# The first two gate/up tiles of each feed-forward layer by the plain product, and the operands of the seven-product form made on VectorE in overlapped chains

## The chip, the cores and the metric

The kernel runs on one core of one Trainium2 chip, as one program. The metric is the device time of one execution in microseconds (us); the median of 3 runs of the kernel before is 3172.42 us (3166.53 to 3172.50).

The engines are named as in the profile: PE is the matrix engine (TensorE), PEld its loading of the fixed operand, DVE the vector engine, ACT the scalar engine with the activation functions, POOL the GpSimd engine, SP the engine whose queue issues most DMA transfers. Each takes its instructions in the order of its own list, and a wait holds up all that stands behind it on that engine. Matrix products are written to PSUM banks, everything else lies in SBUF.

## The reference

One step of a two-layer network over 1024 latent tokens and 128 context tokens, 1152 in all, with 1024 features. Layer 0 mixes tokens by differential attention, layer 1 by a long convolution, and each is followed by the same feed-forward part, which is all that this change touches:

```python
def swiglu(h, w_gu, w_down):
    g, u = jnp.split(h @ w_gu, 2, axis=-1)
    return (jax.nn.silu(g) * u) @ w_down

h = modulate(rmsnorm(xs, norm2_g[i]), sh2, sc2)      # normalised, scaled and shifted by features
xs = xs + g2 * swiglu(h, ffn_w_gu[i], ffn_w_down[i])
```

`w_gu` is 1024 x 5632: 2816 gate columns and 2816 up columns. All is in float32.

## The kernel before, in words

**Precision.** PE multiplies a 32-bit format with a shorter mantissa, so every operand is kept as two parts: `hi`, a copy rounded by ACT, and `lo`, the rest, by a subtraction (`part`, lines 1635 to 1637). A product is three matrix products, hi*hi, lo*hi and hi*lo (`three`, lines 304 to 307).

**The stage.** `gate_up` (line 969) makes silu(gate)*up for 22 tiles of 128 gate columns with their 128 up columns, for each of the two layers, and stores them to DRAM (`d_a`). The 1152 tokens are two halves of 576 and the 1024 features two halves of 512, so that a pair of tiles is a 2x2 block of weights (gate and up by feature halves) times a 2x2 block of activations (feature halves by token halves). From tile 2 on (the loop in line 1141) that block product takes seven products of a 512x128 weight with a 512x576 activation in place of eight, in a Strassen-Winograd form. Line 1002 lists them: the numbers 1 to 7 are the products (`p1` to `p7`), the letters `a`, `b`, `c` the PSUM banks in which they add up. One product is 24 matrix products of 288 columns (4 feature tiles, 2 column halves, 3 parts; `times`, line 962). The loop body is p1, p6, p2, p7, p5, p4, p3.

**Operands.** The seven products need sums of weight blocks (`side_sums`, on POOL) and of activation blocks. `aa` and `bb` are the lower feature half for the first and second token half, `dd` and `ee` the upper one. Needed are, each as hi and lo, all 4x128 features by 576 tokens: `low` (b0, b1: aa and dd, first token half), `right` (t4: bb, second token half, lower features), `ops[3]` (b2: ee, second token half, upper features), and the combinations t2 = ee - (bb - aa), t3 = t2's sum minus aa, t1 = bb - aa, and a second t4 = dd - t2's sum. The combinations overwrite aa, bb, dd and ee in place, so their order matters.

**The opening of the stage** is where the order is written out by hand, and the call of `pin` in line 1193 keeps the order of the code on PE, DVE, ACT and POOL. The activations of the last third of tokens (256 latents and 128 context tokens, chunk c = 2, all in the second token half) still wait for the norm (`rstd_parts`) and for `apply` (line 891: a DVE product with the norm, then scale and shift on ACT, and on POOL for the context columns). Until they are there only the first token half can be multiplied. Therefore tile 0 is done plainly: `gate` and `up` with the first token half, 4 products of 24, then with the second, 4 more. Tile 1 is done by the seven products: its p1 runs beside tile 0's first pass, then the others follow as t2, t3, t1 and t4 come.

**Shared places.** Three PSUM banks of name `pr` go round (`bank`, line 995): the fourth product group waits until the first bank has been read out, by ACT (copy or silu) or by DVE. Weight parts `wh` and `wl` have three buffers each, raw weights two (`side_two`, `side_load`). `kept` (line 1077) holds tile 0's results and has the buffer name t1l, which the lo part of t1 takes later; `early`, of name t1h, holds tile 1's weight sums.

## Time and profile before

| | |
|---|---|
| median of 3 runs | 3172.42 us (3166.53 to 3172.50) |
| the profiled execution | 3174.84 us |
| its span | 3172.9 us |
| PE busy | 3054.7 us, 96% of the span |
| DVE busy | 1914.8 us, 60% |
| ACT busy | 1175.3 us, 37% |
| POOL busy | 1017.6 us, 32% |
| mean granted clock of PE | 0.985 |
| opening of layer 0's gate/up stage (first product of tile 0 to first of tile 2) | 982.18 to 1058.62 us |
| the same in layer 1 | 2355.70 to 2433.40 us |

All times within the program are counted from the start of the span. A row of a timeline gives start, duration, engine, line, operation, output<-inputs by the program's names without buffer numbers, and in brackets the idle time of the engine ahead of it and who ended it. L1636 and L1637 are the ACT and the DVE half of `part`, L1251 is any addition, subtraction or product by `tt`, L893 and L900 are `apply`, L1096 is a silu in `close`, L305 to L307 are the three products. A table by stretches gives, per engine, busy microseconds and in parentheses the number of instructions, then the clock that PE was granted as a share of full speed.

### The profile page before, as it was taken

Reading aid. Unit: us, or ns where it says so; the run is one execution under the profiler, and the core shown is the slowest. Engines: PE = TensorE matmul, PEld = TensorE weight load, DVE = VectorE, ACT = ScalarE, POOL = GpSimd, SP = SyncE. Lnnn points to the kernel's source line nnn. Section 1 sums busy time; section 2 is a strip of 40 time slices with the busy share of each in tenths; the row PEclk is TensorE's granted clock in tenths of the full one; section 3 lists DMA queues with packets and bytes.
Section 4 is the critical chain, followed back from the end, with each engine's and each line's share of the span. In section 5 each row is a group of like instructions: output and inputs, shape, how many; then the busy total and the mean of one; then the engine's idle time right before and its main releaser. Section 6 shows DMA issues by size and latency. Waiting matters only on the chain.

```text
span 3172.9 us, 53324 instructions
## 1 busy us (share of the span) xinstructions
PE 3054.7 (96%) x21370; PEld 2977.7 (94%) x21370; DVE 1914.8 (60%) x3103; ACT 1175.3 (37%) x2264; POOL 1017.6 (32%) x886
## 2 busy tenths in 40 slices
PE   6899999999998899999999999999998999999998
PEld 5679989999998899999999999999998999999998
DVE  7866523888926645445544678876456454545555
ACT  3631123888825322223211443335644222222214
POOL 5744310444424434342000323131244443430003
PEclk9999999999999999999999999999999999999999
DMA  6665352444141222224555223345621222125311
GB/s 247 212 203 189 130 161 85 99 90 90 48 155 42 73 76 71 76 77 137 192 213 192 100 98 119 136 153 187 202 69 52 73 77 76 71 76 185 119 63 67
DMA packets 164495, 379.14 MB, mean 119 GB/s; under 512 B 17391, under 2 KB 80247, under 8 KB 161560
## 3 DMA queue, kind: packets, MB, share of 16 engines
q1 hardware_dynamic: 148872, 353.37, 33.9%
q10 hardware_dynamic: 13968, 17.65, 1.5%
q0 software_dynamic: 1408, 4.72, 0.4%
q8 instruction: 168, 2.75, 0.4%
q14 instruction: 79, 0.65, 0.1%
HBM read 278.94 MB, written 96.73 MB: 118 GB/s over the span
## 4 chain that ended last, share of the span: by engine, by line
PE 81%; DVE 6%; DMA 3%; ACT 2%; issue 2%; POOL 1%; SPq 0%; POOLq 0%; ACTq 0%; DVEq 0%
PE mm L305 13%; PE mm L306 13%; PE mm L307 13%; PE pr L305 10%; PE pr L307 10%; PE pr L306 10%; PE tr L791 4%; PE sc L765 2%; PE sc L766 2%; PE tr L782 2%; PE tr L368 1%; DMA zt<-d_z 1%; ACT xk L900 1%; PE tr L307 1%; PE tr L305 1%
## 5 line engine op out<-in xcount | busy, mean ns | idle before, releaser
L306 PE MATMUL mm<-hs,wh 128*128 128x384 f32 x1632 | 548.3, 336 | 0.4 <-POOL hs L469 0.3
L307 PE MATMUL mm<-hs,wl 128*128 128x384 f32 x1632 | 546.6, 335 | 0.0
L305 PE MATMUL mm<-hs,wh 128*128 128x384 f32 x1632 | 545.9, 336 | 0.0
L863 DVE SCALAR_TENSOR_TENSOR xk<-mm,ada,xk 128x192 f32<-128x192 f32 (+3 forms) x560 | 233.6, 453 | 337.4 <-PE mm L307 331.7
L1251 DVE TENSOR_TENSOR xk<-pr,xk 128x576 f32<-128x576 f32 x204 | 154.0, 755 | 392.7 <-PE pr L307 206.4
L420 POOL TENSOR_TENSOR nacc<-nacc,nsq 128x384 f32<-128x384 f32 x104 | 117.2, 1127 | 665.1 <-ACT nsq L416 663.3
L1251 POOL TENSOR_TENSOR xk<-xk,xk 128x576 f32<-128x576 f32 x96 | 139.1, 1449 | 558.7 <-DVE xk L1251 454.1
L306 PEld LDWEIGHTS mm<-hs,wh 128*128 128x128 f32 x1632 | 306.4, 188 | 4.7 <-issue 2.2
L305 PEld LDWEIGHTS mm<-hs,wh 128*128 128x128 f32 x1632 | 306.1, 188 | 3.4 <-DVE xk L863 1.8
L307 PEld LDWEIGHTS mm<-hs,wl 128*128 128x128 f32 x1632 | 306.5, 188 | 2.1 <-issue 0.6
L1636 ACT ACTIVATE wh<-raw 128x1024 fp32r<-128x1024 f32 x154 | 162.5, 1056 | 369.1 <-PE mm L306 322.7
L1637 DVE TENSOR_TENSOR wl<-raw,wh 128x1024 fp32r<-128x1024 f32 x148 | 186.7, 1262 | 54.6 <-ACT wh L1636 54.3
L1637 DVE TENSOR_TENSOR wl<-xk,wh 128x512 fp32r<-128x512 f32 x160 | 180.0, 1165 | 50.4 <-ACT wh L1636 50.4
L305 PE MATMUL mm<-hh,wh 128*128 128x384 f32 x576 | 193.7, 339 | 2.8 <-ACT hh L527 2.3
L306 PE MATMUL mm<-hl,wh 128*128 128x384 f32 x576 | 194.8, 338 | 0.7 <-DVE hl L528 0.7
L307 PE MATMUL mm<-hh,wl 128*128 128x384 f32 x576 | 195.0, 339 | 0.0
L772 DVE TENSOR_REDUCE nm<-sc 128x1 f32<-128x1152 f32 x128 | 173.6, 1357 | 33.5 <-PE sc L766 33.4
L774 ACT ACTIVATE pr<-sc,nm 128x1152 f32<-128x1152 f32 x128 | 156.6, 1223 | 14.3 <-DVE nm L772 7.6
L1061 ACT ACTIVATE xk<-xk 128x576 f32<-128x576 f32 x40 | 27.4, 686 | 352.2 <-DVE xk L1251 352.2
L765 PE MATMUL sc<-kk,qs 128*128 128x384 f32 x384 | 140.1, 365 | 3.3 <-ACT pr L774 3.3
L791 PE MATMUL tr<-v,at 128*128 128x128 f32 x1152 | 139.4, 275 | 0.5 <-ACT at L786 0.5
L647 POOL TENSOR_TENSOR pr<-pr,al 128x384 f32<-128x384 f32 x64 | 53.6, 837 | 260.1 <-DVE al L643 256.7
(398 smaller groups left out, 8900.2 us busy)
## 6 DMA issues: line engine op xcount, KB each, us to landing
raw<-w_gu SPq DMA_DIRECT2D x88, 512.0 KB, 3.5
araw<-ada_w SPq DMA_DIRECT2D x64, 512.0 KB, 4.0
d_a<-xk SPq DMA_DIRECT2D x84, 288.0 KB, 2.1
raw<-w_down SPq DMA_DIRECT2D x44, 512.0 KB, 3.5
araw<-d_a SPq DMA_DIRECT2D x36, 576.0 KB, 7.5
kk<-d_k SPq DMA_DIRECT2D x16, 1152.0 KB, 8.6
raw<-w_in SPq DMA_DIRECT2D x24, 512.0 KB, 3.4
hl<-ada_w SPq DMA_DIRECT2D x23, 512.0 KB, 6.8
```

The lines of the kernel that those rows point to most:

```text
L305: self.nc.tensor.matmul(out, ah, bh, start=first, stop=False, **kw)
L306: self.nc.tensor.matmul(out, ah, bl, start=False, stop=False, **kw)
L307: self.nc.tensor.matmul(out, al, bh, start=False, stop=last, **kw)
L420: nc.gpsimd.tensor_tensor(out=self.acc[c], in0=self.acc[c], in1=sq, op=ALU.add)
L765: nc.tensor.matmul(sc[:, c, :CH], lhs, kk[:, 0, p, ks], start=True, stop=False)
L772: nc.vector.tensor_reduce(out=nm, in_=sv, axis=AX.XY, op=ALU.max, negate=True)
L774: nc.scalar.activation(e.rearrange("p (a b) -> p a b", a=3), sv, AF.Exp, bias=nm, accum_out=st[hd][3][:, p, qt : qt + 1])
L791: self.nc.tensor.matmul(po[:, :P], at[:, b], v[:, b], start=b == 0, stop=b == 8)
L863: self.nc.vector.scalar_tensor_tensor(out=x, in0=ps[:, s:e], scalar=gate[:, d, g : g + 1], in1=x, op0=ALU.mult, op1=ALU.add)
L1251: (eng or self.nc.vector).tensor_tensor(out=o, in0=a, in1=b, op=op)
L1636: self.nc.scalar.activation(hi, x, AF.Copy)
L1637: (eng or self.nc.vector).tensor_tensor(out=lo, in0=x, in1=hi.bitcast(F32), op=ALU.subtract)
```

## The change

In `gate_up`, for both layers:

- Tile 1 is multiplied plainly too: eight products in place of seven, spread over the two token halves. The first pass over the first token half holds gate and up of tile 0 and gate of tile 1; the second pass holds gate and up of tile 0 on the second half; then come up of tile 1 on the first half, gate of tile 1 on the second, up of tile 1 on the second.
- Tile 1's weight sums (`sums(1)`, four POOL instructions) and their four splits go away, with the buffer `early`; its up weights are split as they are, 128x1024.
- The splits of the weights of tiles 0 and 1 take their lo part on DVE where they had it on POOL. The subtractions bb - aa and dd - ee are on DVE too, and were on POOL.
- The operands are formed by a helper `chain`, which places `apply` of piece j, the ACT copy of piece j-1 and the DVE subtraction of piece j-2 in one round. Silu and product of the finished tiles stand inside these chains at a given round.
- Tile 1's closing work (additions in p6, p7, p5, p4, p3 and the products on POOL) becomes two silus on ACT and two products on DVE; `copies` goes, since only its plain case is left.
- t1 and the second t4 are formed in chains after tile 1's last product. Nothing is changed from `pair(t, 3)` of tile 2 on.

```diff
         raws(0)
-        g11, g12 = self.side_two(st[0]["raw"][0], eng=pool)
-        u21, u22 = self.side_two(st[0]["raw"][1], eng=pool)
+        g = self.side_two(st[0]["raw"][0])
+        u = self.side_two(st[0]["raw"][1])
         raws(1)
-        pair(1, 1, pool)
+        g1 = self.side_two(st[1]["raw"][0])
         norm = self.rstd_parts(NCH - 1)
-        gate, up, one = bank(), bank(), st[1]
-        one["a"] = bank()
-        kept, early = (self.tl(tp, [P, 4, HALF], tag=n) for n in ("t1l", "t1h"))
-        sums(1, [early[:, j, 0:512] for j in range(4)])
+        gate, up, gate1 = bank(), bank(), bank()
+        kept = self.tl(tp, [P, 4, HALF], tag="t1l")
+        low = [ops[1], ops[2]]
+
+        def plain(out, w, b, *halves):
+            for n in range(2):
+                self.times(out, w[n], b[n], n == 0, halves or (0, 1))
+
         for h in range(2):
-            self.times(gate, g11, ops[1], True, [h])
-            self.times(gate, g12, ops[2], False, [h])
+            plain(gate, g, low, h)
             if h == 0:
                 next(norm)
-            self.times(up, u21, ops[1], True, [h])
-            self.times(up, u22, ops[2], False, [h])
+            plain(up, u, low, h)
             if h == 0:
                 rs = next(norm)
-            self.times(one["a"], one["w"][1], ops[1], True, [h])
+            plain(gate1, g1, low, h)
...
-        for k in range(4):
-            apply(NCH - 1, k, rs)
-        for k in range(4):
-            self.part(*act(right, k), bb[k])
-            tt(bb[k], bb[k], aa[k], LESS, pool)
-            apply(NCH - 1, k + 4, rs)
-        close(0, gate, up)
-        copies(one, "s1", AF.Copy, "nacc", 3)
-        for k in range(4):
-            self.part(*act(ops[3], k), ee[k])
-        gate, up = bank(), bank()
-        self.times(gate, g11, right, True)
-        self.times(up, u21, right, True)
-        self.times(gate, g12, ops[3], False)
-        self.times(up, u22, ops[3], False)
-        for k in range(4):
-            tt(ee[k], ee[k], bb[k], LESS)
-            self.part(*act(t2, k), ee[k])
-        pair(1, 2)
-        for k in range(4):
-            tt(aa[k], ee[k], aa[k], LESS)
-            self.part(*act(t3, k), aa[k])
-        for k in range(4):
-            tt(dd[k], dd[k], ee[k], LESS, pool)
-        close(1, gate, up)
-        pair(1, 3, pool)
+        def silu(n, ps):
+            nc.scalar.activation(flat(kept, n), ps, AF.Silu)
+
+        def close(t, n, ps):
+            tt(flat(kept, n), ps, flat(kept, n), MUL)
+            store(t, n % 2, flat(kept, n))
+
+        def chain(dst, src, pre=None, lag=1, at={}):
+            n = len(src)
+            for j in range(n + 2 * lag):
+                if j < n and pre:
+                    pre(j)
+                k = j - lag
+                if 0 <= k < n:
+                    nc.scalar.activation(dst[k][0], src[k], AF.Copy)
+                k -= lag
+                if 0 <= k < n:
+                    tt(dst[k][1], src[k], dst[k][0].bitcast(F32), LESS)
+                if j in at:
+                    at[j]()
+
+        def rows(*ops):
+            return [(t[0][:, k], t[1][:, k]) for t in ops for k in range(4)]
+
+        chain(rows(*high), bb + ee, lambda k: apply(NCH - 1, k, rs), 1, {5: lambda: silu(0, gate), 8: lambda: close(0, 0, up)})
+        silu(2, gate1)
+        gate, up = bank(), bank()
+        plain(gate, g, high)
+        plain(up, u, high)
+        u1 = self.side_two(st[1]["raw"][1])
+        raws(2)
+        for k in range(4):
+            tt(bb[k], bb[k], aa[k], LESS)
+        chain(rows(t2), ee, lambda k: tt(ee[k], ee[k], bb[k], LESS), 1, {2: lambda: silu(1, gate), 4: lambda: close(0, 1, up)})
+        ups = bank()
+        plain(ups, u1, low)
+        gate1 = bank()
+        plain(gate1, g1, high)
+        pair(2, 1)
+        chain(rows(t3), aa, lambda k: tt(aa[k], ee[k], aa[k], LESS), 1, {4: lambda: close(1, 2, ups)})
+        sums(2)
+        silu(3, gate1)
+        ups = bank()
+        plain(ups, u1, high)
+        pair(2, 2)
+        for k in range(4):
+            tt(dd[k], dd[k], ee[k], LESS)
+        pair(2, 4)
+        close(1, 3, ups)
         ops[6], ops[7] = t2, t3
-        p2(1, "nsq", 2)
-        p6(1)
         ops[5] = self.operand(tp, "t1")
-        for k in range(4):
-            self.part(*act(ops[5], k), bb[k])
-        p7(1)
-        pair(1, 4, pool)
-        raws(2)
+        chain(rows(ops[5]), bb)
         ops[4] = self.operand(tp, "t4")
-        for k in range(4):
-            self.part(*act(ops[4], k), dd[k])
-        p5(1), sums(2), pair(2, 1)
-        p4(1), pair(2, 4), pair(2, 2)
-        p3(1), raws(3)
+        chain(rows(ops[4]), dd)
+        raws(3)
```

The lines of the changed kernel below line 1004 have other numbers: what is L1637 before is L1635 there, L1251 is L1249, and the copies and silus of the new helpers are L1098 and L1085.

Three places show how instructions moved, all in layer 0. The first is ACT at the end of the first pass, where t4h and b2h are the hi parts of the second token half, L900 is the scaling of a piece, and t1l is `kept`, with the silu that frees tile 0's gate bank (pr_10940). Before:

```order
L1636 ACTIVATE t4h_11096<-xk_9912 128x576
L900 ACTIVATE xk_9928<-xk_9928,ada_136_214,A_2112_9986 128x256
L1636 ACTIVATE t4h_11096<-xk_9916 128x576
L900 ACTIVATE xk_9932<-xk_9932,ada_136_214,A_2112_9986 128x256
L1636 ACTIVATE t4h_11096<-xk_9920 128x576
L900 ACTIVATE xk_9936<-xk_9936,ada_136_214,A_2112_9986 128x256
L1636 ACTIVATE t4h_11096<-xk_9924 128x576
L900 ACTIVATE xk_9940<-xk_9940,ada_136_214,A_2112_9986 128x256
L1096 ACT_TABLE_LOAD
L1096 ACTIVATE t1l_10943<-pr_10940 128x576
L1016 ACTIVATE nacc_11139<-pr_10942 128x288
```

And in the change:

```order
L900 ACTIVATE xk_9920<-xk_9920,ada_136_214,A_2112_9986 128x256
L1098 ACTIVATE t4h_11115<-xk_9916 128x576
L900 ACTIVATE xk_9924<-xk_9924,ada_136_214,A_2112_9986 128x256
L1098 ACTIVATE t4h_11115<-xk_9920 128x576
L900 ACTIVATE xk_9928<-xk_9928,ada_136_214,A_2112_9986 128x256
L1098 ACTIVATE t4h_11115<-xk_9924 128x576
L900 ACTIVATE xk_9932<-xk_9932,ada_136_214,A_2112_9986 128x256
L1098 ACTIVATE b2h_11117<-xk_9928 128x576
L1085 ACT_TABLE_LOAD
L1085 ACTIVATE t1l_10943<-pr_10940 128x576
L900 ACTIVATE xk_9936<-xk_9936,ada_136_214,A_2112_9986 128x256
L1098 ACTIVATE b2h_11117<-xk_9932 128x576
```

Between the scaling of a piece and its copy stands one other scaling now (three before), and the silu with its table load stands ahead of the last two scalings and of three copies, where it stood behind all scalings and ahead of the b2h copies.

The second place is DVE at t2, in the same layer (xk_9928 and the next three are ee, xk_9912 and the next three bb). Before:

```order
L1251 TENSOR_TENSOR xk_9928<-xk_9928,xk_9912 128x576
L1637 TENSOR_TENSOR t2l_11093<-xk_9928,t2h_11092 128x576
L1251 TENSOR_TENSOR xk_9932<-xk_9932,xk_9916 128x576
L1637 TENSOR_TENSOR t2l_11093<-xk_9932,t2h_11092 128x576
L1251 TENSOR_TENSOR xk_9936<-xk_9936,xk_9920 128x576
L1637 TENSOR_TENSOR t2l_11093<-xk_9936,t2h_11092 128x576
```

And in the change:

```order
L1249 TENSOR_TENSOR xk_9928<-xk_9928,xk_9912 128x576
L1249 TENSOR_TENSOR xk_9932<-xk_9932,xk_9916 128x576
L1249 TENSOR_TENSOR xk_9936<-xk_9936,xk_9920 128x576
L1249 TENSOR_TENSOR t2l_11112<-xk_9928,t2h_11111 128x576
L1249 TENSOR_TENSOR xk_9940<-xk_9940,xk_9924 128x576
L1249 TENSOR_TENSOR t2l_11112<-xk_9932,t2h_11111 128x576
```

The subtraction that needs ACT's copy of a piece no longer follows the one that makes the piece; two others stand between.

The third place is POOL at the start of the stage, where nacc is the sum of squares for the norm of the last tokens and wl the lo part of weights. Before:

```order
L1637 TENSOR_TENSOR wl_10925<-raw_10920,wh_10924 128x1024
L420 TENSOR_TENSOR nacc_10086<-nacc_10086,nsq_10772 128x384
L1637 TENSOR_TENSOR wl_10929<-raw_10921,wh_10928 128x1024
L420 TENSOR_TENSOR nacc_10086<-nacc_10086,nsq_10874 128x384
L1637 TENSOR_TENSOR wl_10937<-raw_10932,wh_10936 128x1024
L420 TENSOR_TENSOR nacc_10086<-nacc_10086,nsq_10905 128x384
```

And in the change:

```order
L420 TENSOR_TENSOR nacc_10086<-nacc_10086,nsq_10772 128x384
L420 TENSOR_TENSOR nacc_10086<-nacc_10086,nsq_10874 128x384
L420 TENSOR_TENSOR nacc_10086<-nacc_10086,nsq_10905 128x384
```

The three weight splits left this list for that of DVE, where each stands between two splits of activations.

More of the change, by code (lines that the diff above doesn't have):

```diff
@@ L1005, in mul @@
             self.times(q[name], q["w"][n], ops[n], first)
-        def copies(q, name, func, tag=None, bufs=None):
-            if tag is None:
-                q[name] = [(slice(0, 2), work())]
-            else:
-                q[name] = []
-                for h in range(2):
-                    y = self.tl(self.np_, [P, CH], tag=tag, bufs=bufs)[:, 0:SUB]
-                    q[name].append((slice(h, h + 1), y.rearrange("p (a b) -> p a b", a=1)))
-            for h, y in q[name]:
-                nc.scalar.activation(y, q["a"][:, h], func)
         def store(t, h, y):
@@ L1022, in p1, with p2 @@
             mul(t, 1)
-            copies(st[t], "s1", AF.Copy)
-        def p2(t, *where):
+            st[t]["s1"] = work()
+            nc.scalar.activation(st[t]["s1"], st[t]["a"], AF.Copy)
+        def p2(t):
             mul(t, 2)
-            copies(st[t], "g", AF.Silu, *where)
+            st[t]["g"] = work()
+            nc.scalar.activation(st[t]["g"], st[t]["a"], AF.Silu)
         def p6(t):
@@ L1032, in p6 @@
             q["v"] = work()
-            for h, y in q["s1"]:
-                tt(q["v"][:, h], q["b"][:, h], y, ADD)
+            tt(q["v"], q["b"], q["s1"], ADD)
         def p7(t):
```

21 lines of the change are left out of this document (7 added, 14 removed).

## The prediction, made before the changed kernel ran

> **What bounds the kernel now.** I read the head of the page and the chain that ended last first, then a table of busy times by stretches (both openings, part of the loop, 20 us of it).
>
> ```profile
> span 3172.9 us, 53324 instructions
> PE 81%; DVE 6%; DMA 3%; ACT 2%; issue 2%; POOL 1%; SPq 0%; POOLq 0%; ACTq 0%; DVEq 0%
> ```
>
> ```profile
> 982.18:1058.62 76.44, 58.84 (x373) 56.90 (x374) 55.97 (x88) 38.35 (x75) 37.90 (x32) 0.87 0.09 32
> 1058.62:1500.00 441.38, 441.38 (x3327) 441.38 (x3326) 219.57 (x225) 117.04 (x187) 176.47 (x118) 1.00 0.25 86
> 2355.70:2433.40 77.70, 59.90 (x376) 57.96 (x375) 55.73 (x90) 39.29 (x76) 38.92 (x32) 0.85 0.09 31
> 1060.00:1080.00 20.00, 20.00 (x153) 20.00 (x152) 11.40 (x13) 5.66 (x10) 8.89 (x8) 1.00 0.37 130
> ```
>
> PE carries 81% of the chain. Inside the loop of the gate/up stage it never rests (441.38 of 441.38 us at clock 1.00), and a product costs 20.00/153 = 0.1307 us. The openings, which this change rewrites, are different: PE works 58.84 of 76.44 us in layer 0 and 59.90 of 77.70 in layer 1, at clocks of 0.87 and 0.85. How many products are in there is told by the weight loads (the second count) for the banks `pr` in layer 0, since some matmul records are missing:
>
> ```profile
> 982.18:1058.62 76.44, 56.59 (x359) 54.82 (x360) 4.63 (x8) 2.58 (x6) 0.00 (x0) 0.87 0.09 32
> ```
>
> 360 products at 0.1307 are 47.1 us, in layer 1 the same. The opening takes 77.07 in the mean of both layers, so 30 us per layer are lost, to waits and to a slow PE. PE's waits in layer 0:
>
> ```profile
> PE pr L305 <- ACT t1l L1096: 11.9, 2, 7.5
> PE tr L455 <- DVE ndg L454: 2.1, 1, 2.1
> PE pr L306 <- DVE b1l L1637: 2.0, 1, 2.0
> PE pr L306 <- DVE t4l L1637: 1.4, 2, 0.7
> PE pr L305 <- DVE xk L863: 0.7, 1, 0.7
> PE tr L435 <- POOL nacc L420: 0.3, 1, 0.3
> ```
>
> ```profile
> 987.69 0.40 PE L306 MATMUL pr<-b1l,wh 128*128 128x288 f32 x1 [1.96 <-DVE b1l L1637]
> ...
> 990.04 0.44 PE L306 MATMUL pr<-b0l,wh 128*128 128x288 f32 x1
> 990.28 0.44 PE L307 MATMUL pr<-b0h,wl 128*128 128x288 f32 x1
> ...
> 996.29 1.78 PE L455 MATMUL tr<-ndg,ones 128*128 128x128 f32 x6 [2.09 <-DVE ndg L454]
> ...
> 1012.92 0.40 PE L305 MATMUL pr<-t4h,wh 128*128 128x288 f32 x1 [4.40 <-ACT t1l L1096]
> ...
> 1038.07 0.61 PE L305 MATMUL pr<-t2h,wh 128*128 128x288 f32 x1 [7.46 <-ACT t1l L1096]
> ```
>
> The waits sum to some 18 us. The other 12 are slow products: after the 1.96 and 0.33 us of rest they come 0.24 us apart (990.04, 990.28) instead of 0.13. For one such stretch:
>
> ```profile
> 989.25:994.19 4.94, 4.94 (x26) 4.71 (x25) 4.93 (x13) 4.94 (x14) 4.37 (x4) 0.65 0.00 0
> ```
>
> It holds 24 products and one more record or two; 4.94 - 24 x 0.1307 = 1.8 us lost at a granted clock of 0.65. That is my price of one slow stretch, about once per wait of 2 us and more.
>
> The two largest waits end at a silu on ACT (L1096), which empties a PSUM bank that PE wants. It is not slow, it stands late in ACT's list:
>
> ```profile
> 1010.92 1.28 ACT L1096 ACT_TABLE_LOAD   x1
> 1012.22 0.65 ACT L1096 ACTIVATE t1l<-pr 128x576 f32<-128x576 f32 x1
> ```
>
> PE had ended its pass at 1012.92 - 4.40 = 1008.5, and the last 36 products of the pass are for other banks, so this gate bank was full by 1008.5 - 36 x 0.1307 = 1003.8. The silu ran 8 us later, behind the scalings and copies of the whole t4 chain. That chain goes one piece at a time, DVE to ACT to ACT to DVE (rows of these two engines):
>
> ```profile
> 1002.07 0.55 DVE L893 TENSOR_TENSOR xk<-tr,xk 128x384 f32<-128x384 f32 x1
> 1002.65 0.60 ACT L900 ACTIVATE xk<-xk,ada,A 128x256 f32<-128x256 f32 x1 [1.29 <-DVE xk L893]
> 1003.16 0.67 ACT L1636 ACTIVATE t4h<-xk 128x576 fp32r<-128x576 f32 x1
> 1003.86 0.84 DVE L1637 TENSOR_TENSOR t4l<-xk,t4h 128x576 fp32r<-128x576 f32 x1 [1.25 <-ACT t4h L1636]
> 1004.62 0.55 DVE L893 TENSOR_TENSOR xk<-tr,xk 128x384 f32<-128x384 f32 x1
> ```
>
> A round takes 1004.62 - 1002.07 = 2.55 us, about half of it idle on each engine. The 7.46 us have the same form with t3's chain ahead of the silu.
>
> **The change part by part.** *Products.* Tile 1 takes 8 products of 24 instead of 7: 384 x 0.1307 = 50.2 us, 3.1 more per layer. This is certain and on PE's path.
>
> *Operand chains and early silus.* In the new lists a round holds one DVE product, one scaling, one copy and one split of different pieces. ACT is the longer: 0.60 + 0.67 = 1.27 us, against 0.55 + 0.84 on DVE. Eight rounds and two to drain at 1.3 replace eight at 2.55. Where nothing else holds them, splits go at 2.77/4 = 0.69 (rows of DVE and POOL):
>
> ```profile
> 1014.07 2.77 DVE L1637 TENSOR_TENSOR b2l<-xk,b2h 128x576 fp32r<-128x576 f32 x4 [0.41 <-ACT b2h L1636]
> 1017.64 1.44 POOL L1251 TENSOR_TENSOR xk<-xk,xk 128x576 f32<-128x576 f32 x1 [5.92 <-DVE xk L1251]
> 1018.26 1.44 DVE L1637 TENSOR_TENSOR t2l<-xk,t2h 128x576 fp32r<-128x576 f32 x1 [0.75 <-ACT t2h L1636]
> ```
>
> I laid the new lists out by hand from the first product (t = 0), each instruction behind its engine's list and its inputs, with such durations. The norm is there at t = 11, so the first scaling starts near 11.6; ten rounds of 1.3 and the 1.9 of table load and silu, which stand inside, give 26.5 for the first upper-feature operand that PE could miss, b2l. PE ends the first pass at 26.2 and wants b2l at 29.3, after 24 products with t4. ACT's silu has freed its bank at 22.4, since it stands after the sixth round only. The second pass ends at 38.7, up of tile 1 on the first half at 45.0, gate on the second at 51.3, up at 57.5; tile 2's p1, p6, p2 and p7 at 70.1. The later bank waits have slack: the silu of the second pass is through at 40.2 for 45.0, the close at 43 for 51.3. So both waits on L1096 come out at 0. What hides the first silu is the 48 products behind the gate's in the pass (6.3 us); what hides the second is the up tile (6.3 us). If that cover fails, PE waits as in rival one.
>
> *DVE instead of POOL.* DVE takes four weight splits at 1.26 and eight subtractions at 0.75, and loses tile 1's sums and their splits: some 5 us more. It was busy 55.97 of 76.44, and 61 would fill the whole opening of the sum below, were it not that its times have waits for POOL in them. Its weight split, from the page, and then rows of DVE and POOL:
>
> ```profile
> L1637 DVE TENSOR_TENSOR wl<-raw,wh 128x1024 fp32r<-128x1024 f32 x148 | 186.7, 1262 | 54.6 <-ACT wh L1636 54.3
> ```
>
> ```profile
> 980.34 3.28 POOL L1637 TENSOR_TENSOR wl<-raw,wh 128x1024 fp32r<-128x1024 f32 x1 [1.17 <-ACT wh L1636]
> 980.36 1.02 DVE L1637 TENSOR_TENSOR b1l<-xk,b1h 128x384 fp32r<-128x384 f32 x2
> 983.63 4.01 DVE L1637 TENSOR_TENSOR b1l<-xk,b1h 128x384 fp32r<-128x384 f32 x2
> ```
>
> The same pair of splits takes 1.02 and 4.01 us; POOL's next weight split runs in the second. The t2l split takes 1.44 beside POOL's, 0.69 without. So some 5 us come back, and the chains of t1 and the second t4 now lie beside tile 2's first four products. In the layout DVE has 19 us left in the opening and is not the bound.
>
> *Norm.* Its first half was asked of PE at 988.56 (6.4 after the start, behind POOL), its second came 7.7 later. In the change the first half is asked after 24 products and with POOL free, at t = 3.2: the second half at 3.2 + 7.7 = 11 at the latest, while PE is done with its products at 7 or 8. The wait is between 0 and 4; I take 2.4, near today's 2.09, since DVE has three weight splits more in its list there. It brings one slow stretch, 1.8.
>
> In a sentence that the sum can do without: the Trainium skill, "TensorE: Matmul & The Clock Gate", Part 1, has the clock fall only after idle gaps of more than about 3 us, by which 2.4 would cost no slow stretch and the total would be 2 x 1.8 = 3.6 us lower. This case's rows disagree: the slow stretch at 0.65 follows gaps of 1.96 and 0.33.
>
> *New wait.* t1l is `kept`'s buffer, so t1's lo part waits for the last store of tile 1 (2.1 us on the queue), which waits for the last close. With t1, t4 and the last weight split behind it on DVE, p5 of tile 2 has its operands at about t = 71.5, when PE asks at 70.1:
>
> ```profile
> d_a<-xk SPq DMA_DIRECT2D x84, 288.0 KB, 2.1
> ```
>
> I take 1.5; 0 if DVE is quicker, 5 if it is as loaded as today.
>
> *Sum per layer:* 50.2 products, 1.6 for the norm's own small products (58.84 - 56.59 = 2.2 today, partly at the slow clock), 2.4 norm wait, 1.8 slow clock, 0.5 for a later start (0 to 1; ACT and DVE have more ahead of the first product), 1.0 of small waits in the layout: 57.5 to the first product of tile 2. With 1.5 at p5 it is 59.0. The same layout of the old lists gave 74.1 and 75.9, short of the measured 76.44 and 77.70 by 2 in round numbers, so I take 61.0. Saved: 77.07 - 61.0 = 16.1, in two layers 32. The profiled execution took 3174.84, which is 2.4 over the median of the runs: 3174.84 - 32.2 = 3142.6, on the median 3140.
>
> **The rivals.**
> *One: the second operand chain stays late.* ACT's table load and silu stand inside it; if its rounds stay near 2.55, ten of them from 11.6 with 1.9 end at 39 instead of 26.5, but only the b2 half is missed, and the first four are needed at 26.2, so PE waits some 6 us in the second pass (half of the 12.5) and is slow for 1.8 more: 61 + 8 = 69, saved 16 in all, 3156. For it: ACT waited for DVE in every round above (1.29). Against: that wait comes from the order in the lists, which is what changes.
>
> *Two: p5 of tile 2 waits longer,* for the store and t1: 3 us more and a slow stretch, 65.8 per layer, saved 22.5, 3150. For it: everything stands in one line behind the last close. Against: PE has 96 products meanwhile.
>
> *Three: every wait goes,* the norm's too: 50.2 + 1.6 + 1 = 52.8, saved 48.5, 3124. Against: the norm's 7.7 us lie mostly in its own steps, and its first half can't be asked sooner.
>
> *Four: no effect.* The 16 us saved would have to be waited for again at a fixed point behind, such as a transfer. The loop that follows runs at full PE, and no row shows one.
>
> *Five: slower.* The loop starts with DVE late: t1 and t4 are made after tile 1, and tile 2's sums, raw weights and splits come behind them. If this lag is handed from tile to tile, each of some 40 tiles stalls PE at its p5. It decides from 32/40 = 0.8 us per tile; at 1.5 it costs 60 and the opening's 32 don't cover it: 3172 + 28 = 3200. Against: in the loop DVE is busy 219.57 and POOL 176.47 of 441.38 us, so about half of each tile's time is free to work off a lag, and 5 us are gone in a tile or two.
>
> **How the numbers follow.** Forecast 0.66; rival one 0.12, two 0.10, three 0.05, four 0.03, five 0.04. The forecast's own range per layer: norm -4.2 (no wait, no slow stretch) to +1.6, start 0.5 either way, p5 -1.5 to +3.5, correction 2 either way; taken as independent, -4.9 to +4.4, the two layers alike, so 3130 to 3149. Reaching to rivals one and two above and toward three below, 3127 to 3158 leaves out 2 in 10. A measurement of this kernel tells changes over about 0.2%, 6 us, from none: faster 0.93, same 0.03, slower 0.04.
>
> **What would show it.** Right: 384 weight loads for `pr` in each opening, no wait on the silu over 1 us, one norm wait near 2.4 with one slow stretch behind it, openings of about 59 us to tile 2's first product, a wait under 2 at its p5, chain rounds of 1.3 us, DVE's splits of weights near 1.26 and no wl on POOL before the first product, and the loop still full. Wrong: an opening over 66 (the place of the wait tells the rivals apart), PE below 99% in the loop, or a slow stretch with no wait ahead of it, by which my price of waits falls.

## The result, and the profile after

| | before | changed kernel |
|---|---|---|
| median of 4 runs | 3171.74 us (3166.53 to 3172.50) | 3143.60 us (3140.97 to 3150.18) |
| ratio, with its 95% interval | | 0.9918 (0.9898 to 0.9937) |
| the profiled execution | 3174.84 us | 3150.18 us |
| its span | 3172.9 us | 3148.3 us |

The forecast was 3140 us in a range of 3127 to 3158, with a saving of 32 us. The medians differ by 28.1 us, the two profiled executions by 24.7; the profiled one of the changed kernel is the longest of its four runs.

The head of the page of the changed kernel. PE has 48 more products (24 per layer), POOL 55 us less work, and DVE's busy time is a little lower than before (1914.8) although it has eight instructions more:

```profile
span 3148.3 us, 53347 instructions
PE 3051.0 (97%) x21418; PEld 2977.4 (95%) x21418; DVE 1901.2 (60%) x3111; ACT 1171.4 (37%) x2248; POOL 962.2 (31%) x842
```

The table by stretches of the changed kernel has layer 0's opening (first product of tile 0 to first of tile 2), then tile 2 of layer 0 up to the first product of tile 3, then layer 1's opening, then part of the loop:

```profile
980.93:1037.13 56.20, 54.46 (x398) 54.07 (x399) 43.49 (x83) 33.42 (x64) 15.18 (x14) 0.97 0.17 55
1037.13:1066.79 29.66, 24.83 (x171) 24.59 (x170) 18.09 (x21) 7.54 (x13) 7.92 (x5) 0.88 0.21 68
2343.42:2402.40 58.98, 56.02 (x401) 55.33 (x400) 45.32 (x86) 34.64 (x66) 16.74 (x14) 0.94 0.16 54
1066.79:1480.00 413.21, 413.21 (x3116) 413.21 (x3115) 203.48 (x206) 108.78 (x173) 165.74 (x109) 1.00 0.23 80
```

The openings took 76.44 and 77.70 us and take 56.20 and 58.98 now, with 24 more products each. The second row is new: tile 2 took 22.30 us in the kernel before, with PE busy throughout, and takes 29.66 here. For comparison, the same stretch of the kernel before:

```profile
1058.65:1080.95 22.30, 22.30 (x171) 22.30 (x170) 12.75 (x14) 5.66 (x10) 10.67 (x9) 1.00 0.36 121
```

So the account is this. From the first product of tile 0 to the first of tile 3, layer 0 went from 98.77 to 85.86 us and layer 1 from 99.99 to 88.76, which saves 12.9 + 11.2 = 24.1 of the 24.6 us by which the spans differ. Everything else cancels to half a microsecond: the first opening begins 1.2 us earlier, what lies between tile 3 of layer 0 and the opening of layer 1 is 1.9 longer, and what comes behind is 1.1 shorter.

What PE waits for in layer 0's stage now, to be held against the 11.9, 2.1, 2.0, 1.4, 0.7 and 0.3 us of before:

```profile
PE pr L305 <- DVE xk L1249: 4.8, 1, 4.8
PE tr L455 <- DVE ndg L454: 1.7, 2, 1.5
PE pr L305 <- DVE xk L863: 1.6, 1, 1.6
```

Both waits on the silu are gone, and so are those on b1l and t4l. The wait on the norm stayed, and there is one of 4.8 us that did not exist. The 1.6 us of the last row lie ahead of the first product, outside the stretch. The timeline of PE shows where they lie:

```profile
989.84 0.68 PE L455 MATMUL tr<-ndg,ones 128*128 128x128 f32 x4 [1.46 <-DVE ndg L454]
990.81 0.49 PE L455 MATMUL tr<-ndg,ones 128*128 128x128 f32 x2 [0.28 <-DVE ndg L454]
...
1054.98 0.61 PE L305 MATMUL pr<-t1h,wh 128*128 128x288 f32 x1 [4.83 <-DVE xk L1249]
```

The last row is the first product of p5 of tile 2. Between 991.05 and 1050.14 PE makes 432 products without a wait.

One round of the operand chain in the changed kernel (rows of DVE and ACT):

```profile
996.99 0.67 ACT L1098 ACTIVATE t4h<-xk 128x576 fp32r<-128x576 f32 x1
997.03 0.55 DVE L893 TENSOR_TENSOR xk<-tr,xk 128x384 f32<-128x384 f32 x1
997.61 0.60 ACT L900 ACTIVATE xk<-xk,ada,A 128x256 f32<-128x256 f32 x1
997.69 0.77 DVE L1249 TENSOR_TENSOR t4l<-xk,t4h 128x576 fp32r<-128x576 f32 x1
998.38 0.55 DVE L893 TENSOR_TENSOR xk<-tr,xk 128x384 f32<-128x384 f32 x1
```

From one product with the norm to the next it is 998.38 - 997.03 = 1.35 us, where it was 2.55.

The wait at p5 is explained by what DVE, SP and POOL do ahead of it. DVE and SP's queue:

```profile
1038.32 0.74 DVE L1249 TENSOR_TENSOR t1l<-pr,t1l 128x576 f32<-128x576 f32 x1
1043.28 6.50 DVE L1249 TENSOR_TENSOR t1l<-xk,t1h 128x576 fp32r<-128x576 f32 x4 [4.21 <-DMA d_a<-t1l]
1049.70 2.75 DVE L1249 TENSOR_TENSOR t4l<-xk,t4h 128x576 fp32r<-128x576 f32 x4
...
1054.18 1.41 DVE L1249 TENSOR_TENSOR xk<-pr,xk 128x576 f32<-128x576 f32 x2
```

```profile
1038.42 0.33 SPq L936 DMA_DIRECT2D raw<-w_gu  x1
1039.09 0.33 SPq L1008 DMA_DIRECT2D d_a<-t1l  x1
```

POOL meanwhile:

```profile
1042.58 1.28 POOL L1249 TENSOR_TENSOR xk<-raw 128x512 f32<-128x512 f32 x1 [8.01 <-DMA raw<-w_gu]
1043.94 1.69 POOL L1249 TENSOR_TENSOR xk<-xk,raw 128x512 f32<-128x512 f32 x1
1045.59 1.80 POOL L1249 TENSOR_TENSOR xk<-raw,raw 128x512 f32<-128x512 f32 x1
1047.35 1.81 POOL L1249 TENSOR_TENSOR xk<-raw,xk 128x512 f32<-128x512 f32 x1
```

DVE closes tile 1 at 1038.32 and then stands for 4.21 us until the store of that result has left the buffer (`kept`) which t1's lo part takes next. By then the raw weights of tile 3 have landed and POOL's sums begin, and the four splits of t1l, 0.69 us each where nothing else runs, take 6.50. Behind them stand t4l, three splits of weights, and only then the addition at 1054.18, which reads p6's result out of the PSUM bank in which p5 adds up. PE is not waiting for t1 itself at the end, but for an addition that is queued behind it.

The store is late because a load stands ahead of it in SP's queue. The two rows of that queue are the load of raw weights (512 KB), issued at 1038.42, and the store (288 KB), issued 0.67 us behind it. In the trace's record of DMA packets the load's run from 1039.39 to 1042.08 and the store's from 1041.33 to 1042.80, so the store begins 2.24 us after its issue. The three stores of the same buffer and size before it, issued at 1005.72, 1022.24 and 1029.39, each begin 0.82 us after their issue. The times show this; no run moved the load.

### The profile page after: what moved, and what is told of

Read it like the earlier page. It is cut to its first block, busy times and chain, and to the rows that moved or that the text cites. A ratio compares the mean times of both kernels' runs of the same rounds, so it can differ in the third digit from the quotient of the medians.

```text
span 3148.3 us, 53347 instructions
## 1 busy us (share of the span) xinstructions
PE 3051.0 (97%) x21418; PEld 2977.4 (95%) x21418; DVE 1901.2 (60%) x3111; ACT 1171.4 (37%) x2248; POOL 962.2 (31%) x842
## 3 DMA queue, kind: packets, MB, share of 16 engines
q0 software_dynamic: 1408, 4.72, 0.4%
## 5 line engine op out<-in xcount | busy, mean ns | idle before, releaser
L1249 DVE TENSOR_TENSOR xk<-pr,xk 128x576 f32<-128x576 f32 x200 | 150.7, 754 | 391.9 <-PE pr L307 205.9
L1249 POOL TENSOR_TENSOR xk<-xk,xk 128x576 f32<-128x576 f32 x80 | 116.6, 1457 | 543.4 <-DVE xk L1249 449.3
L1635 DVE TENSOR_TENSOR wl<-raw,wh 128x1024 fp32r<-128x1024 f32 x156 | 197.0, 1263 | 68.4 <-ACT wh L1634 68.1
L1635 DVE TENSOR_TENSOR wl<-xk,wh 128x512 fp32r<-128x512 f32 x160 | 176.9, 1144 | 52.3 <-ACT wh L1634 52.0
L791 PEld LDWEIGHTS tr<-v,at 128*128 128x128 f32 x1152 | 133.8, 192 | 3.1 <-ACT at L786 0.8
```

The lines of the kernel that those rows point to most:

```text
L791: self.nc.tensor.matmul(po[:, :P], at[:, b], v[:, b], start=b == 0, stop=b == 8)
L1249: (eng or self.nc.vector).tensor_tensor(out=o, in0=a, in1=b, op=op)
L1635: (eng or self.nc.vector).tensor_tensor(out=lo, in0=x, in1=hi.bitcast(F32), op=ALU.subtract)
```

## The experiments

The changed kernel is the basis unless another is named. Besides the times, each trace gives the distance from the first product of tile 0 to the first of tile 2 and to the first of tile 3 (worked out by counting PE's weight loads):

| | median us | to tile 2, layer 0 / 1 | to tile 3, layer 0 / 1 |
|---|---|---|---|
| before | 3171.7 | 76.5 / 77.7 | 98.8 / 100.0 |
| changed kernel | 3143.6 | 56.2 / 59.0 | 85.9 / 88.8 |
| last result in buffers of its own | 3131.0 | 54.7 / 59.0 | 77.0 / 81.3 |
| no overlap in the chains | 3160.5 | 60.0 / 61.8 | 94.4 / 95.4 |
| silus and closes behind the chains | 3145.0 | 56.2 / 57.9 | 85.6 / 87.7 |
| weight splits back on POOL | 3150.6 | 59.8 / 60.7 | 88.7 / 90.5 |
| bb - aa, dd - ee back on POOL | 3144.8 | 54.7 / 57.9 | 83.0 / 86.3 |
| before, with overlapped chains | 3144.4 | 63.6 / 63.6 | 85.9 / 86.3 |
| the same, weight splits on DVE | 3144.1 | 59.9 / 62.4 | 82.2 / 84.6 |
| the same, reordered | 3145.1 | 61.9 / 63.9 | 84.2 / 86.2 |
| own buffers, norm asked later | 3129.5 | 53.5 / 54.9 | 75.8 / 77.2 |
| the same, three more edits of order | 3127.1 | 53.6 / 55.0 | 75.9 / 77.3 |

The rest of the program, outside the two stretches to tile 3, differs by a few microseconds from trace to trace, above all in when the first opening begins (977.8 to 985.6 us). Differences of 3 us between medians are therefore read from the stretches.

**The last result of tile 1 in other buffers.** Only the last silu, product and store of tile 1 leave `kept`, for two half-size buffers of the norm's:

```diff
+            for h in range(2):
+                last.append(self.tl(self.np_, [P, CH], tag="nsq", bufs=2)[:, 0:SUB])
+                nc.scalar.activation(last[h], ps[:, h], AF.Silu)
...
+                tt(last[h], ps[:, h], last[h], MUL)
+                nc.sync.dma_start(self.d_a[l][t][:, HALF + SUB * h : HALF + SUB * h + SUB], last[h])
```

> The changed kernel, but the last result of tile 1 (silu, product and store) goes into two buffers of 288 columns of the norm's, not into the buffer that the lo part of t1 takes next; so t1 no longer waits for that store. Theory (the store is what makes p5 of tile 2 late): PE's wait there, 4.8 us in layer 0 and 5.0 in layer 1, falls to under 0.5, and the slow products behind it (2.3 us per layer) go too; some 14 us saved over both layers, about 3130 us. Rival (DVE is late anyway, since POOL's sums for tile 3 run beside its splits, 6.50 us for the four that take 2.75 alone): the wait stays at 2.5 or more, at most 6 us saved, 3138 or more.

Measured: 3131.03 us, ratio 0.9871 (0.9857 to 0.9886). Tile 2 of layer 0 takes 22.30 us again, as it did before:

```profile
1036.37:1058.67 22.30, 22.30 (x171) 22.30 (x170) 14.76 (x22) 7.69 (x13) 9.96 (x5) 1.00 0.27 87
```

DVE and POOL in this kernel (L1261 is L1249 of the changed one):

```profile
1038.29 2.75 DVE L1261 TENSOR_TENSOR t1l<-xk,t1h 128x576 fp32r<-128x576 f32 x4
1040.96 2.76 DVE L1261 TENSOR_TENSOR t4l<-xk,t4h 128x576 fp32r<-128x576 f32 x4
```

```profile
1041.96 4.72 POOL L1261 TENSOR_TENSOR xk<-raw 128x512 f32<-128x512 f32 x1 [8.14 <-DMA raw<-w_gu]
```

The theory holds: the store was what made p5 late, and the interference with POOL came on top only because DVE had been made to wait until POOL began. With DVE already running, all eight splits go at 0.69 and POOL's first sum is the one that is stretched, to 4.72 us; PE does not wait at p5.

**No overlap in the chains.**

```diff
-        chain(rows(*high), bb + ee, lambda k: apply(NCH - 1, k, rs), 1, {5: lambda: silu(0, gate), 8: ...
+        chain(rows(*high), bb + ee, lambda k: apply(NCH - 1, k, rs), 0, {4: lambda: silu(0, gate), 7: ...
```

and the same lag of 0 in the chains of t2 and t3.

> The changed kernel with the chains not overlapped: each piece is applied, copied and split before the next begins; silus and closes stay behind the same piece. Theory (the overlap feeds the second pass): rounds of about 2.5 us again, the last upper operand some 8 us later than in the changed kernel (1006.4 in layer 0), PE waits 3 to 4 us in the second pass and loses 1.8 to the slow clock, and p5 of tile 2 comes 5 us later still; 15 to 20 us over both layers, about 3160. Rival (the gain comes from the early silus alone, which free the PSUM banks): no new wait, within 3 us of the changed kernel's 3143.6.

Measured: 3160.50 us, ratio 0.9966 (0.9953 to 0.9978), so 16.9 of the 28 us are given back. PE's waits in layer 0:

```profile
PE pr L305 <- DVE xk L1249: 7.0, 1, 7.0
PE pr L305 <- ACT t1l L1085: 3.3, 1, 3.3
PE pr L305 <- ACT xk L1013: 2.0, 1, 2.0
```

The second row is the bank of the second pass, as expected (1.9 us in layer 1). The third was not foreseen: the copy of tile 2's p1, which ACT does behind its late copies. And p5's wait grew by 2.2 us in layer 0 and 0.5 in layer 1, not by 5. The size of the sum was right, its parts only in direction. The overlap carries most of the gain.

**Silus and closes behind the chains.** The entries in braces are taken out of the three chains, and the same calls stand behind them.

```diff
-        chain(rows(*high), bb + ee, lambda k: apply(NCH - 1, k, rs), 1, {5: lambda: silu(0, gate), 8: ...
+        chain(rows(*high), bb + ee, lambda k: apply(NCH - 1, k, rs))
+        silu(0, gate)
+        close(0, 0, up)
```

> The changed kernel with the overlapped chains, but the silus and products of finished tiles behind each chain, not inside. Theory (overlap is what counts): the silu of tile 0 ends near 1004.8 in layer 0's time, PE wants its bank at 1005.6, so no wait over 0.5 us; the second one has 6 us of slack; within 3 us of 3143.6. Rival (the early silus are what counts): the waits of 4.4 and 7.5 us on the silu come back at least by half, 10 to 20 us over both layers, 3155 or more.

Measured: 3144.97 us, ratio 0.9917 (0.9902 to 0.9932). PE has no wait on a silu in either layer, and the openings are 56.2 and 57.9. Where the silus stand does not matter once the chains are short: the first silu was late before because 2.55 us per piece were ahead of it, not because it stood behind the chain. An early silu with long chains was tried in the run before this one, where PE still waits 3.3 us for it.

**The weight splits back on POOL.**

```diff
-        g = self.side_two(st[0]["raw"][0])
-        u = self.side_two(st[0]["raw"][1])
+        g = self.side_two(st[0]["raw"][0], eng=pool)
+        u = self.side_two(st[0]["raw"][1], eng=pool)
...
-        g1 = self.side_two(st[1]["raw"][0])
+        g1 = self.side_two(st[1]["raw"][0], eng=pool)
```

> The changed kernel with the lo parts of the first three weight splits (gate and up of tile 0, gate of tile 1) back on POOL. Theory (POOL's long splits hold up DVE's splits of the first activations): the wait of 2.0 us on b1l, with some 1.8 us of slow products behind it, is back in each layer, less the 1 us by which the first product can start sooner; 4 to 7 us over both layers, 3148 to 3151. Rival (that DVE has three splits more ahead of the first product costs as much as POOL's interference): within 2 us of 3143.6.

Measured: 3150.61 us, ratio 0.9935 (0.9917 to 0.9953), 7.0 us more than the changed kernel. The old picture is back, PE waiting for b1l behind a pair of splits that takes 4.01 us beside POOL (rows of DVE, POOL and PE):

```profile
981.05 4.01 DVE L1635 TENSOR_TENSOR b1l<-xk,b1h 128x384 fp32r<-128x384 f32 x2
981.97 2.67 POOL L1635 TENSOR_TENSOR wl<-raw,wh 128x1024 fp32r<-128x1024 f32 x1
...
985.11 0.40 PE L306 MATMUL pr<-b1l,wh 128*128 128x288 f32 x1 [1.96 <-DVE b1l L1635]
```

In the changed kernel the same pair takes 1.01. The openings are 3.6 and 1.7 us longer, the stretches to tile 3 2.8 and 1.7. So this move is the second part of the gain, 7.0 us by the medians and 4.5 by the stretches.

**bb - aa and dd - ee back on POOL.**

```diff
-            tt(bb[k], bb[k], aa[k], LESS)
+            tt(bb[k], bb[k], aa[k], LESS, pool)
...
-                tt(dd[k], dd[k], ee[k], LESS)
+                tt(dd[k], dd[k], ee[k], LESS, pool)
```

> The changed kernel with bb - aa and dd - ee back on POOL. Theory (they are off the path here: POOL is idle when bb - aa is due, and the store that t1 waits for decides p5 of tile 2): PE's waits as in the changed kernel, within 3 us of 3143.6. Rival (the move to DVE brought part of the gain, since POOL takes 1.44 us for each and slows DVE's splits meanwhile): a wait of 2 us or more ahead of p6 or p7 of tile 2, or p5's wait 2 us longer; 3148 or more.

Measured: 3144.78 us, ratio 0.9915 (0.9894 to 0.9935), in runs from 3137.2 to 3150.5. No new wait appears; p5's wait is shorter, 3.2 and 3.4 us for 4.8 and 5.0. This part of the change brings nothing, and by the stretches it may cost 2 to 3 us per layer while the store decides; the times are too far apart to tell.

**The kernel before with overlapped chains.** Tile 1 stays at seven products and POOL keeps its weight splits. `chain` forms t4 and b2 in one call and t2 and t3 in two, with the silus inside, and the second pass finishes gate first:

```diff
-        for k in range(4):
-            self.part(*act(right, k), bb[k])
-            tt(bb[k], bb[k], aa[k], LESS, pool)
-            apply(NCH - 1, k + 4, rs)
-        close(0, gate, up)
+        chain(rows(right, ops[3]), bb + ee, lambda k: apply(NCH - 1, k, rs), 1, {5: lambda: silu(0, gate), 8: lambda: close(0, up)})
...
+        for k in range(4):
+            tt(bb[k], bb[k], aa[k], LESS)
+        chain(rows(t2), ee, lambda k: tt(ee[k], ee[k], bb[k], LESS), 1, {2: lambda: silu(1, gate), 4: lambda: close(1, up)})
+        pair(1, 2)
+        chain(rows(t3), aa, lambda k: tt(aa[k], ee[k], aa[k], LESS))
```

> The kernel before, with tile 1 still by seven products and POOL's splits and sums as they were, but t4/b2 and t2, t3 formed in overlapped chains with the silus inside, bb - aa on DVE, and the gate's second pass finished ahead of up's. Theory (overlap and early silus bring the gain, the eighth product only pays for slack): both waits on the silu go, the norm's waits of 2.0 and 2.1 stay; p6, p7, p5 and p4 of tile 1 wait some 4 us together for t2, t3, t1 and the second t4; opening 62 to 66 us instead of 76.4 and 77.7, 3144 to 3150. Rival (without the plain tile 1 the operands come too late): waits of 8 us and more ahead of p6 to p4 of tile 1, opening 70 or more, 3158 or more.

Measured: 3144.38 us, ratio 0.9914 (0.9899 to 0.9928): with none of the plain tile's 48 products it is as fast as the whole change. PE's longest waits in layer 0:

```profile
PE pr L306 <- DVE b1l L1645: 2.0, 1, 2.0
PE pr L305 <- ACT t1h L1644: 1.9, 1, 1.9
PE pr L306 <- DVE t3l L1259: 1.2, 2, 0.9
PE tr L455 <- DVE ndg L454: 1.1, 2, 1.0
```

So the plain tile was no condition of the 28 us. It has none of the short waits on t3 and t1 and pays 24 products of 0.1327, 3.2 us per layer, for it; what it gained then went into p5 of tile 2, which does not wait in this kernel. With that wait out of the way the plain tile is ahead: 3131.0 us in the first experiment, against 3144.1 to 3145.1 for the three versions by seven products.

**The same with the weight splits on DVE.**

```diff
-        g11, g12 = self.side_two(st[0]["raw"][0], eng=pool)
-        u21, u22 = self.side_two(st[0]["raw"][1], eng=pool)
+        g11, g12 = self.side_two(st[0]["raw"][0])
+        u21, u22 = self.side_two(st[0]["raw"][1])
...
-        pair(1, 1, pool)
+        pair(1, 1)
```

> The kernel before with overlapped chains, tile 1 by seven products (3144.4 us), and now the lo parts of the first three weight splits on DVE as in the change. Theory (POOL's splits hold up DVE's): the wait of 1.95 us on b1l and its slow products (about 1.8) go, the start is 1 us later; 3 us saved per layer, 3138. Rival (DVE's extra splits make the norm later in turn): the wait on the norm grows by what b1l's shrinks; within 2 us of 3144.4.

Measured: 3144.13 us, ratio 0.9912 (0.9894 to 0.9929): no gain in the time. The trace has both theory and rival in it. The wait on b1l is gone, and the norm's wait has grown from 1.1 to 2.7 us:

```profile
PE tr L455 <- DVE ndg L454: 2.7, 2, 2.5
```

The openings are 3.7 and 1.3 us shorter all the same, but this trace's first opening begins 7.8 us later than that of the run it is compared with, of which about 1 us is the edit's (PE waits 1.6 us ahead of the first product, where it was 0.7). With runs of one kernel 5 us apart, a gain of this size is not settled here.

**The same, reordered.** The norm's second half is asked after tile 1's 12 products, the second pass goes lower, lower, upper, upper, the first silu a round earlier, and two pieces change place:

```diff
-        chain(rows(t2), ee, ..., 1, {2: lambda: silu(1, gate), 4: lambda: close(1, up)})
+        chain(rows(t2), ee, ..., 1, {2: lambda: silu(1, gate)})
         pair(1, 2)
+        close(1, up)
+        pair(1, 3, pool)
         chain(rows(t3), aa, ...)
         for k in range(4):
             tt(dd[k], dd[k], ee[k], LESS, pool)
-        pair(1, 3, pool)
```

> Tile 1 by seven products with everything the other runs taught: overlapped chains, the first three weight splits on DVE, the norm's second half asked after tile 1's 12 products, the second pass in the order lower, lower, upper, upper, the first silu a round earlier, the second close behind t2's chain, and the split of w5 and w3 ahead of dd - ee on POOL. Theory (384 products were no condition of the gain, they only bought slack, and the slack can be had by order): the waits of 2.5 and 3.8 us on the norm and 1.9 on t1h go or fall under 0.5 each, 360 products stay, 6 us less than the best version with 384 (3127.1), 3121 to 3125. Rival (24 products less mean that t2, t3, t1 and the second t4 are late by as much): PE waits 3 us or more per layer ahead of p6 to p4 of tile 1; 3127 or more.

Measured: 3145.08 us, ratio 0.9909 (0.9892 to 0.9925). The theory missed by 20 us. The wait on t1h went, as meant, but PE waits 4.4 us for t3l in each layer, and DVE's rows (first fence) beside POOL's (second) say why:

```profile
1023.93 1.96 DVE L1260 TENSOR_TENSOR t3l<-xk,t3h 128x576 fp32r<-128x576 f32 x1
1025.81 1.97 DVE L1260 TENSOR_TENSOR xk<-xk,xk 128x576 f32<-128x576 f32 x1
```

```profile
1018.41 3.06 POOL L1646 TENSOR_TENSOR wl<-t1h,wh 128x512 fp32r<-128x512 f32 x2 [12.17 <-ACT wh L1645]
1021.44 7.60 POOL L1260 TENSOR_TENSOR xk<-xk,xk 128x576 f32<-128x576 f32 x4
```

POOL's splits and dd - ee now run from 1018 to 1029 without a break, right beside t3's chain, and each DVE instruction, 0.69 to 0.75 us alone, takes 1.96. What the reordering took off one wait it put on another. Whether seven products can match the plain tile with dd - ee on DVE or later on POOL was not tried.

**The norm asked later.** On the kernel with the last result in its own buffers (3131.0 us), one edit:

```diff
             plain(up, u, low, h)
-            if h == 0:
-                rs = next(norm)
             plain(gate1, g1, low, h)
+            if h == 0:
+                rs = next(norm)
```

> The kernel with the last result in buffers of its own (3131.0 us), and only the norm's second half asked of PE after tile 1's 24 products; the second pass, the first silu and bb - aa are where the change has them. Theory (the best version's 4 us came from this edit alone): the norm's waits of 1.7 and 2.7 us go, at most 1 us is waited for the first silu, the last upper operand (1006.4 in the changed kernel's time, some 0.8 later here) is in time; 3126 to 3129. Rival (the other three edits are needed to cover the second pass): a wait of 1.5 us or more in the second pass in each layer, with slow products behind it; 3130 or more.

Measured: 3129.49 us, ratio 0.9865 (0.9850 to 0.9879), and in another run with three edits more:

```diff
-        plain(gate, g, high)
-        plain(up, u, high)
+        for n in range(2):
+            self.times(gate, g[n], high[n], n == 0)
+            self.times(up, u[n], high[n], n == 0)
...
-        u1 = self.side_two(st[1]["raw"][1])
-        raws(2)
         for k in range(4):
             tt(bb[k], bb[k], aa[k], LESS)
+        u1 = self.side_two(st[1]["raw"][1])
+        raws(2)
```

with the first silu in round 4 for 5.

> The kernel with the last result in buffers of its own (3131.0 us) with four edits of order: the norm's second half is asked of PE only after tile 1's gate product, the second pass goes gate, up by the lower features, then gate, up by the upper ones, the first silu stands a round earlier, and bb - aa stands ahead of the split of tile 1's up weights. Theory (PE can do its 24 products while the norm is finished, and the order gives the upper operand 3.2 us more): the norm's waits of 1.7 and 2.7 us go with the slow products behind them, 3.5 and 5 us per layer, a wait of under 1 us at the first silu's bank remains; 3122 to 3125. Rival (the wait only moves behind the operands of the second pass, whose time the norm sets): PE waits 2 to 4 us there, within 3 us of 3131.

Measured: 3127.07 us, ratio 0.9860 (0.9845 to 0.9876). Both have the same openings to a tenth of a microsecond (53.5 and 54.9; 53.6 and 55.0), so by the stretches the later question to the norm does it alone: 1.2 us in layer 0 and 4.1 in layer 1. The medians of the two differ by 2.4 us, less than the rest of the program varies from trace to trace, and each is a little above what was expected (3126 to 3129, and 3122 to 3125). The wait did not move behind the second pass. What PE still waits for in layer 1 of the faster one:

```profile
PE pr L305 <- ACT t1l L1088: 0.7, 1, 0.7
PE tr L435 <- POOL nacc L420: 0.3, 1, 0.3
PE tr L455 <- DVE ndg L454: 0.2, 1, 0.2
```

384 products at 0.1327 are 51.0 us and the norm's own products about 2, so this opening has 1 to 2 us left in it. At 3127.1 us it is the fastest version of this study, 44.6 us below the kernel before in the medians.

## Why the prediction was right, and where it was off

**What bounds it, and the two silus: right.** The waits of 4.40 and 7.46 us vanished, and with them the slow products behind them. The reason given, that the chain of operands ahead of the silu is what is late, is shown by the two experiments on the chains: without overlap the first wait is back at 3.3 us, and with overlap the silus may stand behind the chains at no cost. So of the two causes that the prediction took together, the overlap and the early place of the silus, the first alone carried it. Nor was the up tile needed to hide the second silu: tile 1 by seven products with overlapped chains has no such tile there, and PE does not wait for a silu.

**Products: 0.1307 was a little low.** It came from 153 matmuls in 20 us, a stretch short enough for its edges to count; 441.38/3327 = 0.1327 was in the same table. 384 products are 51.0 us, not 50.2.

**Norm: right.** Taken as 2.4 us, measured 1.74 (1.46 + 0.28) and 2.72, each with a slow stretch behind it in this trace, of 1.6 and 2.2 us where 1.8 was taken. That the shorter one had a slow stretch at all is chance, as the last section shows.

**The opening to tile 2: right in the layout, not with the allowance.** The layout gave 57.5, the traces have 56.2 and 59.0. The 2 us added because the same layout fell short for the old lists were not needed: the new lists have no long waits that it could underrate.

**DVE in place of POOL: right in sign.** It was costed at nothing, five more microseconds of work against as many of interference, with DVE off the bound. Up to tile 3 of layer 0 DVE is busy 61.58 us with 103 instructions, where it was 68.75 with 101. (In the opening alone it falls from 55.97 to 43.49, but the chains of t1 and the second t4 have moved out of it.) Moving the weight splits is worth 4.5 us over both layers by the stretches and 7 by the medians, through the wait on b1l, which the sum had dropped without a word of its own.

**The new wait at p5 of tile 2: the mis-sized term.** The place and the mechanism were named, the store of `kept` in t1l's way, and 1.5 us was taken, with 5 as the bound. Tile 2 takes 29.66 us for 22.30, so it cost 7.4 in layer 0, of which 4.83 are the wait and about 2.5 the slow products behind; in layer 1 it is 5.01 and 7.5 in all. The wait reached the upper bound and the slow stretch was not in the sum at all. The bound was drawn from a transfer of 2.1 us. But 4.2 us went by from the store's issue (1039.09) to DVE's next instruction, since the store's packets began 2.24 us after the issue, behind a load of 512 KB, and not 0.82 after it. The lateness pushed t1's splits into POOL's sums (6.50 us for 2.75), and the bank of p5 hung on an addition queued behind all of it. That is the second rival as it was worded (3 us more and a slow stretch, 65.8 per layer): measured are 56.20 + 7.36 = 63.6 and 58.98 + 7.5 = 66.5.

**The sum.** 61.0 per layer was forecast and 63.6 and 66.5 were measured, so 24.1 us were saved in place of 32 in the profiled executions. The medians moved by 28.1, because the changed kernel's profiled execution lies 6.6 us over its median and that of before 3.1; so the median came within 3.6 of the forecast although the sum saved 8 too much. That nearness is luck: less than half of the error of the sum is left in it, and the mechanism at p5 was that of the second rival, priced at 3150.

**The rivals.** The late second chain, as far as PE is concerned, did not come; it came when the overlap was taken out. No effect and slower are excluded by the interval of the ratio, 0.9898 to 0.9937. No wait was handed on through the loop: PE is busy 413.21 of 413.21 us behind tile 3. Losing every wait, the third rival at 3124, is what the best version nearly does at 3127.

**The clock.** A slow stretch of 1.8 us for each wait of about 2 was the price used. It was near the mark for this kernel's own waits on the norm (1.6 and 2.2) and low for those at p5 (2.4 and 2.3), but it is no rule: what a wait costs depends on where it lies, as the last section shows.

## What to carry to other kernels

Where PE waits for a short instruction that stands late in an engine's list, look at what is ahead of it before moving it: shortening the chain ahead (one piece's copy beside the next one's product) was worth 17 us, and with the chain short, moving the short instruction was worth nothing. When a result's buffer is taken over by the next operand, the time to cost is not the transfer's alone, but what stands ahead of it in the DMA queue and all that is queued behind the instruction that waits for it, down to the one that reads a PSUM bank out. And an extra product paid for slack pays only if nothing else takes the slack up: here 48 products bought no more than the same overlap did without them, until the last result left the buffer that t1 needed; then the version with them was 13 us faster than the one without that also has its weight splits on DVE (3131.0 for 3144.1; 8.5 us by the stretches to tile 3). The two differ in the order of their lists too, so what the slack alone is worth is not shown.

## What the runs showed of the hardware that was not expected

**DVE and POOL take turns, and it matters who is in possession.** Four splits of 0.69 us took 6.50 when POOL's sums had begun first (1042.58 against 1043.28), and each of POOL's sums was stretched too, from 1.28 to as much as 1.81. Where DVE had begun first, its eight splits went at full speed back to back, and POOL's first sum took 4.72 us, from 1041.96 to 1046.68; DVE's run of instructions ended at 1046.2. In layer 1 of that run it was the same, 4.90 us. That a DVE instruction with two inputs in SBUF and a POOL instruction that reads SBUF lock each other out, and that the order of issue decides which one blocks, is what the Trainium skill says ("SBUF — State Buffer", section "Who interferes with whom"), and the traces agree.

**What a wait costs in slow products depends on where it lies, not on its length alone.** After the same wait on the norm in layer 0, 1.46 or 1.47 and 0.28 us, the changed kernel's products were slow and those of another run were not. The changed kernel, and then the run with bb - aa and dd - ee on POOL, each from the first product behind the wait:

```profile
991.05:995.45 4.40, 4.40 (x23) 4.40 (x23) 3.33 (x9) 4.40 (x12) 1.80 (x3) 0.61 0.02 6
```

```profile
995.09:998.41 3.32, 3.32 (x27) 3.32 (x27) 2.96 (x8) 3.32 (x10) 1.81 (x3) 1.00 0.03 7
```

23 products in 4.40 us at a granted clock of 0.61, against 27 in 3.32 at 1.00. Over all runs, by the distance of the starts of the next 40 products against 0.1327 us each, that wait cost 1.6 us in the changed kernel, 1.4 in the run with late silus, and 0.1 in three others. Waits of 1.9 to 2.1 us cost between 0.1 and 1.6, where no other wait follows within these products, and those of 4 to 7.5 us between 1.5 and 2.9.

The traces' record of the granted clock shows why. In these openings the clock is 1.00 or 0.50, and it changes only at points of a grid of 3.41 us. Stretches of that grid, two of the changed kernel and two of the other run:

```profile
988.44:991.85 3.41, 1.72 (x12) 1.56 (x13) 2.42 (x13) 3.41 (x10) 0.00 (x0) 1.00 0.00 0
991.85:995.27 3.42, 3.42 (x16) 3.42 (x16) 2.64 (x9) 3.42 (x11) 1.80 (x3) 0.50 0.03 7
```

```profile
989.90:993.32 3.42, 2.52 (x20) 2.29 (x18) 3.35 (x17) 3.42 (x10) 0.00 (x0) 1.00 0.18 73
993.32:996.73 3.41, 2.56 (x18) 2.40 (x19) 2.49 (x8) 3.41 (x10) 0.62 (x2) 1.00 0.00 0
```

In the changed kernel both parts of the wait lie, but for 0.06 us, in one window of the grid. PE is busy for 1.72 of its 3.41 us, and the whole next window runs at half the clock. In the other run a point of the grid (993.32) cuts the wait in two, PE is busy for 2.52 and 2.56 us of the two windows, and the clock stays. Counted over 105 us from the window of tile 0's first product, in both layers of all twelve traces, each of the 40 windows at full clock with PE busy for at most 1.725 us was followed by one at half, and each of the 662 with at least 1.754 us by one at full clock. So the line lies near half a window here; over the rest of the program, where PE does other work, busy time does not separate the two. The Trainium skill ("TensorE: Matmul & The Clock Gate", Part 1) describes a free-running window of about 3.4 us in which activity is judged, and the traces agree. Its figure of a window or more of idleness before the clock falls does not agree with 1.46 + 0.28.
